# A transformer block on one core: half of x loaded on ScalarE's queue, the small vectors on GpSimd's

## The chip, the cores and the metric

The kernel runs on one core of a Trainium2 chip. The metric is the device time of one execution in microseconds, the median of several runs. TensorE multiplies matrices; VectorE, ScalarE and GpSimd work element by element; SyncE does little but issue transfers. In the profile they are PE, DVE, ACT, POOL and SP, and PEld is TensorE's weight load. Transfers between the chip's memory and the core run on 16 DMA engines; an instruction on the queue of SyncE, ScalarE or GpSimd issues each one.

## The reference

One decoder block on 256 tokens of width 2048, all in float32. A vector `c` gives six shifts, scales and gates (adaLN).

```python
mod = jax.nn.silu(c) @ w_ada[l] + b_ada[l]
sh1, sc1, g1, sh2, sc2, g2 = jnp.split(mod, 6, axis=-1)
h = modulate(rms_norm(x, norm1_g[l]), sh1, sc1)        # h * (1 + sc1) + sh1
proj = h @ w_in[l]                                     # q, k, v, gb, gc, xt
...
attn = moba_attention(q, k, v)                         # 256 tokens: one causal block
conv = gb * causal_dwconv(gc * xt, conv_w[l], conv_b[l])
mixed = jnp.concatenate([rms_norm(attn, attn_out_g[l]), rms_norm(conv, conv_out_g[l])], axis=-1)
x = x + g1 * (mixed @ w_out[l])
h2 = modulate(rms_norm(x, norm2_g[l]), sh2, sc2)
u = causal_dwconv(h2 @ w_ffn_up[l], ffn_conv_w[l], ffn_conv_b[l])
u_gate, u_up = jnp.split(u, 2, axis=-1)
x = x + g2 * ((jax.nn.silu(u_gate) * u_up) @ w_ffn_down[l])
```

The weights make up nearly all of the 320 MB that are moved: w_ada is 2048 x 12288, w_in 2048 x 6144, w_out 2048 x 2048, w_ffn_up 2048 x 11264 and w_ffn_down 5632 x 2048.

## The kernel before, in words

**Slots.** The program is a list of 205 slots. A slot is one stretch of matmuls on up to four weight blocks of 128 rows by 512 columns: slots 0 to 48 are the input projection, 49 to 64 the output projection, 65 to 204 the feed-forward part, up and down projection in turns. Each float32 weight tile `raw` is loaded by SyncE, copied to a rounded part `hi` by ScalarE (L947) and subtracted to a rest `lo` by VectorE or GpSimd (L958); TensorE multiplies both parts. This split is made two slots ahead of its use.

**Hand-made order.** Nothing is scheduled by a planner at run time: each engine runs its instructions in the order in which the program issues them, and the table `CFG` sets that order by hand. `move` and `cls` say in which slot, and at which place in it, a task stands (an evacuation, a transpose, a piece of attention); `pool` says which `lo` halves of a slot GpSimd makes (1: the first, 2: the second, 3: both, 0: none); `pool_h` names the chunks of `h` whose rest GpSimd makes; `pre`, `mid`, `after` and `carry` say how many steps of adaLN accumulation VectorE does at which place.

**adaLN.** The products with w_ada are spread over the whole program. The first 256 columns of scale and shift (`ada_init`) come first of all: TensorE multiplies each 128 x 256 block with `crep`, a replicated silu(c) (L1034), ScalarE copies the sum out, TensorE transposes it, and VectorE forms the columns A1 and B1 with the first norm's gain and the bias of adaLN, both held in `vbc`.

**The head.** `CFG["start"]` is the order of the first work. In the program's order: c is loaded on ScalarE's queue; constants and the mask are made; x is loaded in four pieces of 128 tokens x 1024 columns, 512 KB each (`xr[t][i]`, L1939, t being the half of the tokens); then the gain of the first norm (16 rows of 128) and the bias of adaLN (96 rows of 128), together `vb` (L854, called at the line after L1939); then the first weight tiles (`load_next`), in the order in which the head uses them: four 512 KB loads of scale columns, eight 256 KB loads of shift columns, then w_in. All but c go through SyncE's queue. ScalarE squares the four pieces of x in the order t = 0, then t = 1 (L1961), VectorE forms 1/rms and scales x in place (L1969), and TensorE transposes it (`xn`, L2029). `vb` is transposed by TensorE to `vbc` between two runs of warm-up matmuls (L1948), ahead of the first `ada` matmuls, and copied out by VectorE after 1/rms. The chunks of h are formed at L1624 to L1631, and the first matmuls of the input projection, `mq`, follow.

**Semaphores of transfers.** The transfers issued by SyncE and ScalarE share eight semaphores, taken in turn: the ninth transfer in the program's order waits, ahead of its issue, until the first has landed. The transfers of GpSimd have eight of their own.

Of the kernel before, what the change touches and what calls it, by code (L numbers as in the profile page):

```python
# [211 lines left out]
               63: 0,  # L212
               64: 6,
               65: 2,
# [20 lines left out]
               108: 3,  # L235
               109: 4,
               159: 2,
               171: 3},
# [56 lines left out]
                72: 0,  # L295
                83: 0},
       'pool_h': [4, 5, 6, 7, 8, 9, 10, 11, 15],
       'psum': [[0, 45]],
# [439 lines left out]
       'evac': [5, 0, 1],  # L738
       'sq': [3, 6, 0],
       'tr': [4, 7, 1],  # L740
# [38 lines left out]
               'qk_root': 0,  # L779
               'evac_out': 1},  # L780
       'la': 2,
       'h_act': True,
       'h_lag': 1,
       'hi_late': [1, 2, 3, 5, 7, 8, 9, 10, 13, 14, 15, 17, 19, 20, 21, 25, 26, 27, 32, 33, 34, 40, 49, 50, 51, 52, 55, 56,
# [3 lines left out]


@with_exitstack  # L790
def tile_block(
# [74 lines left out]
    nc.vector.memset(ones, 1.0)  # L866
    c32 = const.tile([P, P], F32, name="c32")
    nc.vector.memset(c32, 1.0 / 32.0)
    mask = const.tile([P, 384], F32, name="mask")
    nc.gpsimd.memset(mask, 0.0)  # L870
# [70 lines left out]

    def split_hi(nb):
        ts, his = [], []
        for i in range((nb + 1) // 2):
            m = min(2, nb - 2 * i) * 512
            t = take()
            act(piece(his, "hi")[:, :m], t[:, :m], AF.Copy)  # L947
            ts.append((t, m))
        halfway.append((ts, his))
# [36 lines left out]
    class Ada:  # L986


        def __init__(self, part, c0, n, pe, psum=False):
            self.part, self.c0, self.n, self.pe, self.psum = part, c0, n, pe, psum or pe  # L990
            self.rows = 2048 // n
            self.tiles = NK // self.rows
            self.nch = n // P
            self.w = min(n, 512 if self.psum else n)
            self.seen = 0
            self.out = False
            self.own = [] if [part, c0] in CFG["own"] else None

        def want(self, r):
# [12 lines left out]
        def start(self):  # L1012
# [4 lines left out]
            else:  # L1017
                self.acc = [(t4k if self.n > 512 else t2k)(what)[:, :self.n]]

        def consume(self, r, part=None):  # L1020
            if r == 0 and part != 1:
# [4 lines left out]
            for j in range(self.rows) if part is None else range(8 * part, 8 * part + 8):  # L1026
                i = self.rows * r + j
                x = j * self.n % size
                if x == 0:
                    h = take() if self.own is None else self.own.pop(0)  # L1030
                t, last = h[:, x:x + self.n], self.own is None and x + self.n == 1024
                if self.pe:
                    q = 32 * (j % 4)
                    mm(self.acc[0][q:q + 32, :], crep[:, i, :], t,  # L1034
                       start=(r == 0 and j < 4), stop=(r == self.tiles - 1 and j >= self.rows - 4),
                       tile_position=(0, q))
# [40 lines left out]
        def cols(self):  # L1077
# [3 lines left out]
            for a in range(0, self.nch, 4):  # L1081
# [5 lines left out]
                else:  # L1087
# [3 lines left out]
                    V.tensor_reduce(out=z, in_=p[:, :m * P].rearrange("p (k q) -> p k q", q=P), axis=AX.X, op=ALU.add)  # L1091
                self.finish(z, self.c0 + a, m, scale)

        def finish(self, z, c0, m, scale):
# [405 lines left out]
    def evac_down(seg, f):  # L1500
# [3 lines left out]
        for t in range(2):  # L1504
            p = mainp["D", seg, f][t]
            if seg == 0:
                dacc[t, f] = t2k(f"da{t}{f}")
# [10 lines left out]
    def gate_down(f):  # L1518
        assert all(f"ed{seg}{f}" in done for seg in range(len(SEGS) - 1)) and f"un{f}" in done
        done.add(f"gd{f}")  # L1520
        for t in range(2):
            V.tensor_tensor(out=dacc[t, f], in0=dacc[t, f], in1=gB[G2, f], op=ALU.mult)
            V.tensor_tensor(out=x1[t, f], in0=dacc[t, f], in1=x1[t, f], op=ALU.add)

    flip = [False]
# [6 lines left out]
    for seg, (ga, gb_) in enumerate(SEGS):  # L1532
# [50 lines left out]
        for f, k, n in parts:  # L1583
            def go(hi, lo, seg=seg, f=f, k=k, n=n, ka=ka, kb=kb):
                last = k + n == kb
                mm_tok(("D", seg, f), *([blk(v, j) for j in range(n)] for v in (hi, lo)), [gT[k + j] for j in range(n)], n, k == ka, last,
                       last and seg == len(SEGS) - 1)

            slots.append((w_load(w_down, k, n, [(f * 512, 512)]), n, go))
            if k + n == kb:  # L1590
# [7 lines left out]
    ready_at = {}  # L1598

    def spread_loads(g, a, span):  # L1600

        for r in range(g.tiles):
            s = a + r * span // g.tiles
            extra.setdefault(s, []).append((g, r))
        at(s + 1, g.evac)
        if g.gate():
            gates.setdefault(g.part, []).append(g)
# [34 lines left out]
    for i, (g, r) in enumerate(fill):  # L1642
        if i >= n0 + n1 + n2:
            extra.setdefault(N_OUT + (i - n0 - n1 - n2) // 2, []).append((g, r))
        if r == g.tiles - 1:
            a = N_OUT + 1 + max(0, (i - n0 - n1 - n2) // 2)
            at(a, g.evac)
            at(a + 1, g.cols)
            ready_at.update({(g.part, g.c0 + k): a + 1 for k in range(4)})
# [83 lines left out]
    def att_s(h):  # L1733
# [5 lines left out]
        s = t2k("s")[:, :384]  # L1739
        V.tensor_tensor(out=s, in0=p[:, :384], in1=mask, op=ALU.add)  # L1740
        m, z = small(2, "m"), small(2, "z")
        V.reduce_max(out=m[:, 0:1], in_=s[:, :128], axis=AX.X)
        V.reduce_max(out=m[:, 1:2], in_=s[:, 128:], axis=AX.X)
        i, j = (col("q", t, h) for t in range(2))
# [191 lines left out]
    for t in range(2):  # L1936
        xr.append([sb.tile([P, 1024], F32, tag="lo" if t else "hi", bufs=N_HL, name="xr") for _ in range(2)])
        for i in range(2):
            nc.sync.dma_start(xr[t][i], x[0, t * P:(t + 1) * P, i * 1024:(i + 1) * 1024])  # L1939
    vb, nb = rows("vb", [(by_p(norm1_g[0]), 16), (by_p(b_ada[0]), 96)], nc.sync)  # L1940
    for _ in range(N_RAW):
# [53 lines left out]
    def slot(i):  # L1995
        more = i + LA < len(slots)
        hi_late = i == N_OUT or i in CFG["hi_late"]
        if more and not hi_late:
            split_hi(slots[i + LA][1])
        now[0] = i  # L2000
# [5 lines left out]
        if more and hi_late:  # L2006
            split_hi(slots[i + LA][1])
        steps_of(CFG["pre"].get(i, 1))
# [7 lines left out]
        if i > 1:  # L2016
            slots[i][2](*splits.pop(0))
        for g, r in extra.get(i, []):
            g.consume(r)

# [106 lines left out]
```

## Time and profile before

| what | us |
| --- | --- |
| three runs, median (lowest to highest) | 1174.56 (1174.26 to 1174.75) |
| the profiled execution | 1173.49 |
| its span, first to last instruction | 1171.6 |

The profile is of one execution. Its span leaves out what lies before the first and behind the last instruction. "Busy" counts computing instructions; the issue of a transfer isn't counted. A busy TensorE needn't be at its peak, since matmuls overlap. The clock is the share of TensorE's full clock that was granted: its mean over this execution was 0.998.

A row of a timeline is start, length, engine, line, operation, tile written <- tiles read, sizes and count, and in brackets the engine's idle time before it with what ended it. A row of the chain of waits is start, length and what the end was waiting for.

### The profile page before, as it was taken

Reading aid. Unit: us, or ns where it says so; the run is one execution under the profiler, and the core shown is the slowest. Engines: PE = TensorE matmul, PEld = TensorE weight load, DVE = VectorE, ACT = ScalarE, POOL = GpSimd, SP = SyncE. Lnnn points to the kernel's source line nnn. Section 1 sums busy time; section 2 is a strip of 40 time slices with the busy share of each in tenths; the row PEclk is TensorE's granted clock in tenths of the full one; section 3 lists DMA queues with packets and bytes.
Section 4 is the critical chain, followed back from the end, with each engine's and each line's share of the span. In section 5 each row is a group of like instructions: output and inputs, shape, how many; then the busy total and the mean of one; then the engine's idle time right before and its main releaser. Section 6 shows DMA issues by size and latency. Waiting matters only on the chain.

```text
span 1171.6 us, 17108 instructions
## 1 busy us (share of the span) xinstructions
PE 1155.4 (99%) x5989; PEld 965.8 (82%) x5989; DVE 917.6 (78%) x1311; ACT 646.9 (55%) x1002; POOL 169.3 (14%) x100
## 2 busy tenths in 40 slices
PE   7999999999999999999999999999999999999998
PEld 5678888878777878888888888888888888888886
DVE  4469979997788989999999544768888897666785
ACT  4666565578566455556676444555435554445461
POOL 0768673631001021000000000000000000000000
PEclk9999999999999999999999999999999999999999
DMA  9999999995799989986465755576887877875541
GB/s 349 405 405 374 406 353 386 390 388 170 262 368 315 362 272 360 378 276 208 156 207 187 235 180 181 175 230 220 284 299 262 306 245 231 292 246 174 169 155 72
DMA packets 205382, 320.22 MB, mean 273 GB/s; under 512 B 13816, under 2 KB 112300, under 8 KB 205296
## 3 DMA queue, kind: packets, MB, share of 16 engines
q1 hardware_dynamic: 202336, 314.68, 77.2%
q10 hardware_dynamic: 2352, 4.22, 1.3%
q8 instruction: 47, 0.77, 0.3%
q14 instruction: 39, 0.32, 0.1%
q0 software_dynamic: 608, 0.23, 0.1%
HBM read 314.87 MB, written 4.21 MB: 272 GB/s over the span
## 4 chain that ended last, share of the span: by engine, by line
PE 91%; DMA 5%; DVE 3%; issue 1%; ACT 0%; POOL 0%; SPq 0%; DVEq 0%; POOLq 0%; ACTq 0%
PE z L1545 27%; PE z L1549 14%; DMA raw<-in_w_in_dram 2%; DMA raw<-in_w_ada_dram 2%; PE ada L1034 1%; PE mx L1194 1%; PE mx L1196 1%; PE mx L1195 1%; PE mk L1194 1%; DVE ada L1051 1%; PE mg L1194 1%; PE mg L1196 1%; PE mc L1194 1%; PE mq L1194 1%; PE mc L1196 1%; PE mg L1195 1%
## 5 line engine op out<-in xcount | busy, mean ns | idle before, releaser
L947 ACT ACTIVATE hi<-raw 128x1024 fp32r<-128x1024 f32 (+1 forms) x401 | 401.2, 1030 | 314.2 <-PE z L1545 92.9
L958 DVE TENSOR_TENSOR lo<-raw,hi 128x1024 fp32r<-128x1024 f32 x340 | 397.6, 1208 | 95.6 <-ACT hi L947 90.3
L1545 PE MATMUL z<-h,hi 128*128 128x512 f32 x1408 | 328.9, 390 | 0.0
L1545 PEld LDWEIGHTS z<-h,hi 128*128 128x128 f32 x1408 | 261.3, 188 | 52.6 <-DVE h L1440 0.3
L1051 DVE SCALAR_TENSOR_TENSOR ada<-raw,csil,ada 128x512 f32<-128x512 f32 (+2 forms) x215 | 189.0, 892 | 5.6 <-DMA raw<-in_w_ada_dram 2.0
L958 POOL TENSOR_TENSOR lo<-raw,hi 128x1024 fp32r<-128x1024 f32 x61 | 150.5, 2489 | 269.2 <-ACT hi L947 269.2
L1549 PEld LDWEIGHTS z<-h,lo 128*128 128x128 f32 x1408 | 174.8, 192 | 3.4
L1549 PE MATMUL z<-h,lo 128*128 128x256 f32 x1408 | 176.0, 283 | 0.0
L1110 POOL MEMSET gb<- 128x512 f32 x2 | 1.1, 526 | 491.8 <-DVE uy L1484 491.8
L1461 DVE TENSOR_TENSOR ub<-z,ub 128x256 f32<-128x256 f32 x120 | 43.8, 417 | 34.5 <-ACT ub L1458 34.4
L1458 ACT ACTIVATE ub<-z 128x256 f32<-128x256 f32 x120 | 39.7, 383 | 31.1 <-PE z L1545 31.0
L1477 ACT ACTIVATE uy<-ub,vcols 128x256 f32<-128x256 f32 x88 | 45.6, 593 | 6.8 <-DMA gr<-gs 6.7
L1482 DVE SCALAR_TENSOR_TENSOR uy<-ub,vcols,uy 128x255 f32<-128x255 f32 x88 | 42.1, 479 | 5.7 <-ACT uy L1477 5.6
L1484 DVE SCALAR_TENSOR_TENSOR uy<-ub,vcols,uy 128x254 f32<-128x254 f32 x88 | 42.5, 483 | 3.1
L1493 ACT ACTIVATE gh<-uy 128x512 fp32r<-128x512 f32 x22 | 13.9, 630 | 40.6 <-DVE uy L1491 40.6
L1487 ACT ACTIVATE uy<-uy 128x512 f32<-128x512 f32 x22 | 13.9, 633 | 37.2 <-DVE uy L1484 37.2
L1034 PE MATMUL ada<-raw,crep 128*32 128x512 f32 (+1 forms) x224 | 27.1, 525 | 3.2 <-DMA raw<-in_w_ada_dram 2.7
L1494 DVE TENSOR_TENSOR gl<-uy,gh 128x512 fp32r<-128x512 f32 x22 | 15.2, 693 | 17.9 <-ACT gh L1493 17.9
L1194 PE MATMUL mk<-hi,h 128*128 128x512 f32 x64 | 25.8, 403 | 0.0
L1194 PE MATMUL mq<-hi,h 128*128 128x512 f32 x64 | 25.3, 395 | 0.4 <-ACT pa_g L1214 0.4
L1194 PE MATMUL mg<-hi,h 128*128 128x512 f32 x64 | 25.7, 401 | 0.0
L1194 PE MATMUL mx<-hi,h 128*128 128x512 f32 x64 | 25.3, 396 | 0.0
(574 smaller groups left out, 1922.8 us busy)
## 6 DMA issues: line engine op xcount, KB each, us to landing
raw<-in_w_ada_dram SPq DMA_DIRECT2D x180, 512.0 KB, 6.8
raw<-in_w_ffn_up_dram SPq DMA_DIRECT2D x352, 256.0 KB, 4.7
raw<-in_w_in_dram SPq DMA_DIRECT2D x95, 512.0 KB, 7.1
raw<-in_w_ffn_down_dram SPq DMA_DIRECT2D x76, 512.0 KB, 4.7
raw<-in_w_out_dram SPq DMA_DIRECT2D x32, 512.0 KB, 6.1
raw<-in_w_ada_dram SPq DMA_DIRECT2D x24, 256.0 KB, 6.6
raw<-in_w_ffn_down_dram SPq DMA_DIRECT2D x24, 256.0 KB, 3.8
xr<-in_x_dram SPq DMA_DIRECT2D x4, 512.0 KB, 5.4
```

The source lines that it names most:

```text
L947: act(piece(his, "hi")[:, :m], t[:, :m], AF.Copy)
L958: (nc.gpsimd if pool in (i + 1, 3) else V).tensor_tensor(out=piece(los, "lo")[:, :m], in0=t[:, :m], in1=hi[:, :m].bitcast(F32), op=ALU.sub ...
L1034: mm(self.acc[0][q:q + 32, :], crep[:, i, :], t, start=(r == 0 and j < 4), stop=(r == self.tiles - 1 and j >= self.rows - 4), tile_positio ...
L1051: V.scalar_tensor_tensor(out=self.acc[n], in0=v, scalar=csil[:, i:i + 1], in1=acc, op0=ALU.mult, op1=ALU.add)
L1194: mm(o, a, hi[k], start=(first and k == 0 and not seeded), stop=False, skip_group_check=True)
L1458: act(c[ft // 2][:, (ft % 2) * 256:(ft % 2) * 256 + 256], zp[grp][ft][:, 256:], AF.Copy)
L1461: V.tensor_tensor(out=d, in0=zp[grp][ft][:, :256], in1=d, op=ALU.add)
L1477: act(y, b, AF.Identity, bias=fcols[3][:, i:i + 1], scale=fcols[2][:, i:i + 1])
L1482: V.scalar_tensor_tensor(out=y[:, 1:], in0=b[:, :255], scalar=fcols[1][:, i:i + 1], in1=y[:, 1:], op0=ALU.mult, op1=ALU.add)
L1484: V.scalar_tensor_tensor(out=y[:, 2:], in0=b[:, :254], scalar=fcols[0][:, i:i + 1], in1=y[:, 2:], op0=ALU.mult, op1=ALU.add)
L1545: mm(zp[grp][ft], blk(hi, j)[:, ft * P:(ft + 1) * P], h2T[k + j], start=k + j == ks[0], stop=k + j == ks[1] - 1)
L1549: mm(zp[grp][ft][:, :256], blk(lo, j)[:, ft * P:(ft + 1) * P], h2T[k + j][:, :256], start=False, stop=False)
```

## The change

Two issues of x (the second 128 tokens) go from SyncE's queue to ScalarE's, and the two issues of `vb` to GpSimd's. In the same change a number of entries of `CFG` are different, and the code gains branches which the values of `CFG` leave unused (`sets`, `tail`, `lag` empty, `ttr` false). The core of it:

```diff
     for t in range(2):
         xr.append([sb.tile([P, 1024], F32, tag="lo" if t else "hi", bufs=N_HL, name="xr") for _ in range(2)])
         for i in range(2):
-            nc.sync.dma_start(xr[t][i], x[0, t * P:(t + 1) * P, i * 1024:(i + 1) * 1024])
-    vb, nb = rows("vb", [(by_p(norm1_g[0]), 16), (by_p(b_ada[0]), 96)], nc.sync)
+            (nc.scalar if CFG["xq"] and t else nc.sync).dma_start(
+                xr[t][i], x[0, t * P:(t + 1) * P, i * 1024:(i + 1) * 1024])
+    vb, nb = rows("vb", [(by_p(norm1_g[0]), 16), (by_p(b_ada[0]), 96)], nc.gpsimd if CFG["xq"] else nc.sync)
...
+       'xq': True,
+       'lag': {},
+       'sets': [],
+       'tail': [],
+       'ttr': False}
...
-    c32 = const.tile([P, P], F32, name="c32")
+    c32 = const.tile([P, 32], F32, name="c32")
```

The entries of the order table:

```diff
 mid
-               64: 6,
+               148: 2,
 pool
+                153: 3,
+                187: 1,
+                188: 1,
+                189: 1,
+                200: 3},
-       'pool_h': [4, 5, 6, 7, 8, 9, 10, 11, 15],
+       'pool_h': [5, 6, 7, 8, 9, 10, 11, 15],
 after
-                 'evac_in q1 True': 3,
+                 'evac_in q1 True': 1,
 move
+                'evac 2 0': (0, 2),
-                'evac_c 3 1': (0, 1),
+                'evac_c 3 1': (0, 0.5),
-                'ffn_cols': (5, 2),
+                'ffn_cols': (4, 2),
+                'up_conv 10': (0, -2),
-       'sq': [3, 6, 0],
+       'sq': [3, 4, 0],
 hi_late: 66 taken out
```

`mid` is the number of accumulation steps between the two halves of a slot's `lo`; `sq` sets the slot in which a part of the new x is squared (the second part two slots earlier); `ffn_cols` turns the small vectors of the feed-forward part into columns, one slot earlier; `hi_late` lists the slots whose `hi` is made behind the slot's first tasks.

More of the change, by code (lines that the diff above doesn't have):

```diff
@@ L779 @@
                'qk_root': 0,
[L780 removed]
+               'evac_out': 1,
+               'cols_set': -1},
        'la': 2,
@@ L866, in tile_block @@
     nc.vector.memset(ones, 1.0)
-    c32 = const.tile([P, P], F32, name="c32")
+    c32 = const.tile([P, 32], F32, name="c32")
     nc.vector.memset(c32, 1.0 / 32.0)
+    pick = {}
+    for v in (1.0, 1.0 / 32.0):
+        if CFG["sets"]:
+            pick[v] = const.tile([P, 39], F32, name=f"pick{int(1 / v)}")
+            nc.gpsimd.memset(pick[v], 0.0)
+            nc.gpsimd.memset(pick[v][:, 7:8], v)
     mask = const.tile([P, 384], F32, name="mask")
@@ L940, in piece, with split_hi @@
         return t[-1]
-    def split_hi(nb):
+    gated = {}
+    def split_hi(n):
+        nb = slots[n][1]
         ts, his = [], []
@@ L1018, in start, with hold @@
                 self.acc = [(t4k if self.n > 512 else t2k)(what)[:, :self.n]]
+        def hold(self, r):
+            tiles = self.rows * self.n // (1024 if self.own is None else 512)
+            self.held[r] = [take() if self.own is None else self.own.pop(0) for _ in range(tiles)]
         def consume(self, r, part=None):
@@ L1029, in consume @@
                 if x == 0:
-                    h = take() if self.own is None else self.own.pop(0)
+                    src = self.held.get(r, self.own)
+                    h = take() if src is None else src.pop(0)
                 t, last = h[:, x:x + self.n], self.own is None and x + self.n == 1024
@@ L1092, in cols, with cols_set @@
                 self.finish(z, self.c0 + a, m, scale)
+        def cols_set(self):
+            groups = self.set
+            p = bank(f"adas{self.part}_{self.c0}", full=False)
+            parts = [(g, a) for g in groups for a in range(0, g.nch, 4)]
+            for n, (g, a) in enumerate(parts):
+                assert g.out
+                flush(g)
+                e = pick[1.0 / 32.0 if g.pe else 1.0][:, 7 - n:39 - n]
+                m = min(4, g.nch - a)
+                for q in range(m):
+                    mm(p[32 * q:32 * q + 32, :P], e, g.chunk(a + q), start=n == 0, stop=n == len(parts) - 1,
+                       tile_position=(0, 32 * q))
+            r = t1k("adar")[:, :P]
+            act(r, p[:, :P], AF.Copy)
+            p = bank(f"adat{self.part}_{self.c0}", full=False)
+            nc.tensor.transpose(p[:, :P], r, ident)
+            for n, (g, a) in enumerate(parts):
+                m = min(4, g.nch - a)
+                g.finish(p[:, n:n + 32 * m - 31:32], g.c0 + a, m, 1.0)
         def finish(self, z, c0, m, scale):
@@ L1505, in evac_down @@
             p = mainp["D", seg, f][t]
-            if seg == 0:
+            if seg == len(SEGS) - 1 and f in CFG["tail"]:
+                y = t2k(f"d{f}{t}")
+                V.tensor_copy(y[:, :256], p[:, :256])
+                act(y[:, 256:], p[:, 256:], AF.Copy)
+                for eng, a in ((nc.sync, 0), (nc.scalar, 256)):
+                    eng.dma_start(out[0, t * P:(t + 1) * P, f * 512 + a:f * 512 + a + 256], y[:, a:a + 256])
+            elif seg == 0:
                 dacc[t, f] = t2k(f"da{t}{f}")
@@ L1523, in gate_down, with seed_down @@
             V.tensor_tensor(out=x1[t, f], in0=dacc[t, f], in1=x1[t, f], op=ALU.add)
+    def seed_down(f):
+        assert f"gd{f}" in done
+        key = "D", len(SEGS) - 1, f
+        whole[key] = None
+        mainp[key] = [bank(f"ms{f}{t}", keep=True, seed=True) for t in range(2)]
+        for t in range(2):
+            act(mainp[key][t], x1[t, f], AF.Copy)
     flip = [False]
@@ L1587, in go @@
                        last and seg == len(SEGS) - 1)
+            if seg == len(SEGS) - 1 and f in CFG["tail"]:
+                gated[len(slots)] = f
+                if k == ka:
+                    put(len(slots) - 1, CFG["cls_seed"], seed_down, f)
             slots.append((w_load(w_down, k, n, [(f * 512, 512)]), n, go))
@@ L1598, in tile_block, with in_set @@
     ready_at = {}
+    held_until = {}
+    sets = {(part, c0): n for n, e in enumerate(CFG["sets"]) for part, c0 in e}
+    filling = {}
+    def in_set(g, s):
+        n = sets.get((g.part, g.c0))
+        if n is None:
+            return False
+        filling.setdefault(n, []).append((s, g))
+        if len(filling[n]) < len(CFG["sets"][n]):
+            return True
+        s, gs = max(s for s, _ in filling[n]), [g for _, g in filling[n]]
+        gs[0].set = gs
+        at(s + 2, gs[0].cols_set)
+        ready_at.update({(g.part, g.c0 + k): s + 2 for g in gs for k in range(g.nch)})
+        return True
     def spread_loads(g, a, span):
@@ L1604, in spread_loads @@
             extra.setdefault(s, []).append((g, r))
+            lag = CFG["lag"].get(f"{g.part} {g.c0}", 0)
+            if lag:
+                s += lag
+                held_until.setdefault(s, []).append((g, r))
         at(s + 1, g.evac)
+        if in_set(g, s):
+            return
         if g.gate():
@@ L1739, in att_s @@
         s = t2k("s")[:, :384]
-        V.tensor_tensor(out=s, in0=p[:, :384], in1=mask, op=ALU.add)
         m, z = small(2, "m"), small(2, "z")
-        V.reduce_max(out=m[:, 0:1], in_=s[:, :128], axis=AX.X)
-        V.reduce_max(out=m[:, 1:2], in_=s[:, 128:], axis=AX.X)
+        if CFG["ttr"]:
+            for t, a, b in ((0, 0, 128), (1, 128, 384)):
+                V.tensor_tensor_reduce(out=s[:, a:b], in0=p[:, a:b], in1=mask[:, a:b], scale=1.0, scalar=NEG,
+                                       op0=ALU.add, op1=ALU.max, accum_out=m[:, t:t + 1])
+        else:
+            V.tensor_tensor(out=s, in0=p[:, :384], in1=mask, op=ALU.add)
+            V.reduce_max(out=m[:, 0:1], in_=s[:, :128], axis=AX.X)
+            V.reduce_max(out=m[:, 1:2], in_=s[:, 128:], axis=AX.X)
         i, j = (col("q", t, h) for t in range(2))
@@ L1998, in slot @@
         if more and not hi_late:
-            split_hi(slots[i + LA][1])
+            split_hi(i + LA)
         now[0] = i
@@ L2006, in slot @@
         if more and hi_late:
-            split_hi(slots[i + LA][1])
+            split_hi(i + LA)
         steps_of(CFG["pre"].get(i, 1))
@@ L2018, in slot @@
         for g, r in extra.get(i, []):
+            if f"{g.part} {g.c0}" in CFG["lag"] and (g, r) not in fill:
+                g.hold(r)
+            else:
+                g.consume(r)
+        for g, r in held_until.get(i, []):
             g.consume(r)
```

9 lines of the change are left out of this document (8 added, 1 removed), and 6 rows, old and new, of tables.

## The prediction

> **What bounds the kernel now.** I read the page's busy shares and its chain first, then the chain in order of time, then the stretches, then the queues in the first 20 us.
>
> ```profile
> PE 1155.4 (99%) x5989; PEld 965.8 (82%) x5989; DVE 917.6 (78%) x1311; ACT 646.9 (55%) x1002; POOL 169.3 (14%) x100
> PE 91%; DMA 5%; DVE 3%; issue 1%; ACT 0%; POOL 0%; SPq 0%; DVEq 0%; POOLq 0%; ACTq 0%
> 40.50:1168.00 1127.50, 1124.27 (x5781) 945.47 (x5779) 899.17 (x1267) 627.00 (x969) 162.12 (x89) 1.00 0.78 271
> 0.00:40.50 40.50, 31.15 (x210) 20.31 (x211) 17.95 (x44) 19.93 (x33) 7.17 (x12) 0.96 1.00 361
> ```
>
> The last two rows are stretches: bounds, length, then the busy time (and count) of PE, weight loads, DVE, ACT, POOL, the clock, the DMA share, GB/s. From 40.5 us to 1168 us TensorE is busy for 1124.27 of 1127.50 us, so 3.23 us is idle there. In the first 40.5 us, 9.35 us is idle, with the DMA share at 1.00. So the kernel has two parts: a **head** that waits for data, and a **body** in which TensorE runs through. A microsecond gained in the head moves the whole body. The chain of waits (start, length, what) says what the head waits for:
>
> ```profile
> 1.65 6.39 DMA xr<-in_x_dram
> 8.06 7.54 DMA raw<-in_w_ada_dram
> 15.62 6.01 DMA raw<-in_w_in_dram
> 21.65 8.38 DMA raw<-in_w_ada_dram
> 30.05 6.57 DMA raw<-in_w_ada_dram
> 36.66 3.14 PE ada L1034 x16
> ```
>
> Five transfers, end to end, each issued within 0.02 us of the landing of the one before. SyncE's queue issues a load only when an older one has landed; the third piece of x, issued at 1.65, lands at 8.04 and lets a load of w_ada go. From 36.66 on the chain is TensorE. The change acts on the first link.
>
> **The change, part by part.** *The issue.* SyncE's queue in the first microseconds (start, length, engine, what):
>
> ```profile
> 0.74 1.81 SPq L1939 DMA_DIRECT2D xr<-in_x_dram  x4
> 2.59 0.93 SPq L854 DMA_DIRECT2D vb<-in_norm_g_dram  x1
> 3.57 0.46 SPq L854 DMA_DIRECT2D vb<-in_b_ada_dram  x1
> 4.08 11.19 SPq L1007 DMA_DIRECT2D raw<-in_w_ada_dram  x12
> ```
>
> Two of the four x issues and both issues of vb leave this queue, so the first w_ada load goes out where the third x issue stood: at 1.65 in place of 4.08, **2.43 us earlier**. Two of the w_ada loads behind it also lose the x or vb transfer that they waited for. Issue time is not data, though. The stretches show what the DMA engines did with the time:
>
> ```profile
> 0.00:2.00 2.00, 0.00 (x0) 0.00 (x0) 0.31 (x2) 0.81 (x1) 1.32 (x9) 1.00 0.19 18
> 2.00:4.00 2.00, 0.00 (x0) 0.00 (x0) 0.00 (x0) 0.47 (x1) 0.28 (x2) 1.00 0.69 197
> 4.00:6.00 2.00, 1.37 (x6) 1.36 (x7) 0.60 (x2) 0.85 (x2) 0.00 (x0) 1.00 1.05 414
> 6.00:8.00 2.00, 2.00 (x12) 2.00 (x11) 0.00 (x0) 1.96 (x5) 0.00 (x0) 1.00 1.00 297
> 10.00:20.00 10.00, 7.74 (x75) 3.21 (x75) 5.43 (x17) 2.59 (x7) 0.00 (x0) 1.00 1.09 388
> ```
>
> The last column is GB/s. From 10 us on the engines are full at 388 GB/s and stay so through the head; the bytes that the head needs don't change. So the head can move only by bytes carried sooner in the first 8 us. Against 388 GB/s, 2 to 4 us loses (388 − 197)/388 × 2 = 0.98 us, and 6 to 8 us loses (388 − 297)/388 × 2 = 0.47 us. The first 2 us lose 1.91 us, but nothing is issued before 0.74, and I count none of it as won. The thin stretch of 2 to 4 us has all of x issued by 2.55, on one queue, with the engines 69% busy. A second queue that feeds the same engines from about 1.2 us should fill most of it. No trace shows this, so the bounds are wide: nothing (the engines themselves start slowly) and 2.43 us (the whole shift of the issue). I take three quarters of both losses, 0.75 × 1.45 = 1.09, or **1.1 us**, since the third row shows the engines at 414 GB/s right after, with x alone still moving.
>
> A rule of the Trainium skill speaks against this. "DMA: Bandwidth & Descriptors", section "Issuing engines are not separate DMA queues", says that transfers started by different engines run on the same 16 DMA engines and interleave, and that starting them from several engines saves only the time of the sequencer. By that rule alone the sum would be near nothing; the share of 0.69 at 2 to 4 us says the engines still had room, so the trace doesn't settle it.
>
> *What TensorE can use of it.* On the other branch of the head stands x itself:
>
> ```profile
> 5.36 1.28 ACT L1954 ACT_TABLE_LOAD   x1
> 6.77 1.04 ACT L1961 ACTIVATE j<-xr 128x1024 f32<-128x1024 f32 x1
> 10.29 1.06 ACT L1961 ACTIVATE j<-xr 128x1024 f32<-128x1024 f32 x1
> 9.94 0.29 PE L878 MATMUL pv_vbc<-ident,vb 112*128 112x112 f32 x1 [0.49 <-DMA vb<-in_b_ada_dram]
> 10.07 0.62 PE L1948 MATMUL warm<-ones,ident 128*128 128x128 f32 x4
> 13.36 0.81 PE L2029 MATMUL xn<-ident,xr 128*128 128x128 f32 x4 [0.49 <-DVE xr L1969]
> 14.92 0.64 PE L1034 MATMUL ada<-raw,crep 128*32 128x256 f32 x8 [0.18 <-DMA raw<-in_w_ada_dram]
> 16.87 4.14 PE L1034 MATMUL ada<-raw,crep 128*32 128x256 f32 x32
> 16.87 0.58 PEld L1034 LDWEIGHTS ada<-raw,crep 128*32 128x32 f32 x12 [0.17 <-issue]
> 20.38 0.14 PEld L1034 LDWEIGHTS ada<-raw,crep 128*32 128x32 f32 x4 [0.53 <-DMA raw<-in_w_ada_dram]
> ```
>
> The four squares of x run back to back from 6.77 (one each 1.17 us), begun when a table load ends, not when x lands; so the normalized x reaches TensorE at 13.36 whatever x does, unless a piece lands late. Behind it the shift columns' matmuls start at 16.87, or 16.69 without the 0.18 us of DMA wait at 14.92. Twelve weight loads take 0.58 there when the data is present, so the last four of 32 could start at 16.69 + 28 × 0.048 = 18.04 in place of 20.38: TensorE can take in up to **2.3 us**. My 1.1 fits under this cap. The first w_in tile and the w_ada loads up to 36.62 stand in the same full stream and move with it.
>
> *Where the moved issues go.* The rows are ScalarE's and GpSimd's first work, and two on later loads by GpSimd (shortest, median and longest issue in ns; us to landing):
>
> ```profile
> 0.73 0.42 ACTq L854 DMA_DIRECT2D vc<-in_c_dram  x1
> 5.13 0.21 ACT L1953 ACTIVATE csil<-ccol 128x16 f32<-128x16 f32 x1 [2.66 <-DVE ccol L880]
> 1.74 0.54 POOL L872 TENSOR_SCALAR_AFFINE_SELECT mask<-mask 128x128 f32<-128x128 f32 x2
> 34.94 11.82 POOL L958 TENSOR_TENSOR lo<-raw,hi 128x1024 fp32r<-128x1024 f32 x5 [32.66 <-ACT hi L947]
> L854 POOL DMA_DIRECT2D v<-in_norm_g_dram x1: 653/653/653, 66.6 to 66.6; - x1
> DMA to landing us min/median/max: 4.8/5.2/5.5
> ```
>
> ScalarE's two x issues cost 2 × 0.45 (a quarter of SyncE's 1.81 each) after its own load of c, beginning near 1.19, and push its first table load, of 1.28 like the one at 5.36, to end near 3.4. ScalarE is idle until 5.13, so this is hidden; without that cover it would cost 0.9. GpSimd issues vb after its mask, from about 2.3 us; later loads of the same kind show the price. At 0.65 an issue, the second starts at 2.95 and vb lands by 2.95 + 5.5 = 8.5, where TensorE now waits for it until 9.94. What stands in TensorE's order between vb and 13.36 is 0.29 + 0.62 (four warm matmuls) + 2 × 0.64; vb is harmless until 13.36 − 2.19 = 11.2. GpSimd's next work is at 34.94, after 32.66 us without any. Gain from vb itself: 0, as the work behind it waits for w_ada and x.
>
> *The order edits.* The table of pieces that GpSimd subtracts gains one for each of the slots 187 to 189 and two for 153 and for 200, seven in all; one chunk of h goes from GpSimd to VectorE; some tasks and accumulation steps of slots 18 to 66, 125 and 148 move within their slot or by one or two. The entry removed for slot 64 is never read (that slot returns before it). The unused branches (sets, tail, lag, ttr) issue nothing; c32 shrinks from 128 to 32 columns.
>
> ```profile
> L958 DVE TENSOR_TENSOR lo<-raw,hi 128x1024 fp32r<-128x1024 f32 x340 | 397.6, 1208 | 95.6 <-ACT hi L947 90.3
> L958 POOL TENSOR_TENSOR lo<-raw,hi 128x1024 fp32r<-128x1024 f32 x61 | 150.5, 2489 | 269.2 <-ACT hi L947 269.2
> 980.00:1168.00 188.00, 187.01 (x944) 159.66 (x944) 131.23 (x179) 85.72 (x118) 0.00 (x0) 1.00 0.58 186
> 1145.29 0.63 ACT L947 ACTIVATE hi<-raw 128x512 fp32r<-128x512 f32 x1 [1.61 <-PE m('D', 3, 1)1_11131 L1196]
> 1149.17 0.39 PE L1194 MATMUL m('D', 3, 3)0_11295<-hi,gh 128*128 128x512 f32 x1
> ```
>
> A piece takes 2.49 us on GpSimd and 1.21 on VectorE, but is made two slots before it is used. The tightest is slot 200: its second, half-wide piece can start at 1145.92 and ends near 1147.4 (half of 2.49), 1.7 us ahead of its matmuls. So the edits cost 0; if all seven stood on the path they would cost 7 × 1.28 = 9.0 us. What they can win is at most the 3.23 us of TensorE idle time behind 40.5 us. I take 0: none of the idle time is shown to end with one of the moved tasks.
>
> **The sum.** 1.1 us of the profiled execution's 1173.49 (span 1171.6 and 1.9 around it). That execution lies 1.07 us below the median of the runs, 1174.56, so I take the gain from the median: 1174.56 − 1.1 = 1173.46, say **1173.4**. A measurement of this kernel can tell about 0.2%, or 2.35 us, from no change, so this counts as the same.
>
> **The rivals.** *First, the start is the engines' own.* If 2 to 4 us stay thin with two queues, w_ada's earlier issue only lengthens the line behind x, and what is left is at most part of the 0.47 us: about 1174.3. For it: the third row, where the rate reaches 414 with nothing changed but time. Against it: the 69%. The same result comes if the last piece of x, now interleaved with w_ada, lands after 10.29: from there each microsecond late pushes 13.36 and eats the gain.
>
> *Second, the whole shift comes through.* If the 2.43 us of earlier issue arrive as earlier landings, the cap gives 2.3 us, and if a quarter of the later idle time also goes (0.25 × 3.23 = 0.8), the time is 1174.56 − 3.1 = 1171.5. For it: five landings in a row each release the next issue, so that an early first link is handed on. Against: a full stream at 388 GB/s hands on bytes, not issue times.
>
> *Third, slower: a GpSimd piece that comes late.* The place is slots 187 to 200, where seven subtractions go to an engine that takes twice as long. The price is 1.28 us for each that TensorE waits for; from three on the path (3.8 less the 1.1 of the head) the kernel is 2.7 us slower, and at four the time is 1174.56 + 5.1 − 1.1 = 1178.6. It decides when a hi piece ends later than 1.7 us after where it ends now (slot 200). For it: GpSimd does nothing from 980 us to 1168 now, so no row shows such a piece there. Against: the lead of two slots.
>
> The change doing less than it says isn't likely: the code moves the two x issues and vb without condition.
>
> **How the numbers follow.** Forecast (0.5 to 2.2 us won) 0.52; first rival 0.15; second 0.25; third 0.08. The first two of these are within 0.2%, the second rival is faster by over 0.2%, the third slower: faster 0.25, same 0.67, slower 0.08. The range leaves out the third and about half of the second rival: from 1171.2 (the cap of 2.3, 0.8 of later idle time, and 0.3, by which the runs differ from their median) to 1175.2 (no gain, and half of one piece late).
>
> **What would show it.** The first w_ada issue on SyncE's queue at about 1.65; 2 to 4 us well above 197 GB/s; x's squares still from 6.8 us; vb's transpose near 9.5 without a DMA wait; the last shift matmuls and the ada matmuls that begin at 36.66 all about 1.1 us earlier; from 40.5 us on the same 3.2 us of idle time. The forecast is wrong if 2 to 4 us stay at 197, if squares wait for x, or if TensorE's idle time behind 40.5 us changes by more than 1 us.

## The result, and the profile after

| | us | runs |
| --- | --- | --- |
| before, median (lowest to highest) | 1174.47 (1172.72 to 1174.75) | 6 |
| changed, median (lowest to highest) | 1183.09 (1180.92 to 1184.23) | 6 |
| the profiled execution of the changed kernel | 1183.94, span 1182.2 | 1 |

The changed kernel is slower by 0.73%: the ratio is 1.0073, with a 95% interval from 1.0059 to 1.0086, or 8.6 us. That is small, but clear of the scatter of the runs. The forecast was 1173.4 and its range ended at 1175.2.

The page of the changed kernel first: busy time of the engines in us, and the shares of the chain that ended last.

```profile
PE 1158.2 (98%) x5989; PEld 966.6 (82%) x5989; DVE 920.3 (78%) x1305; ACT 646.5 (55%) x1002; POOL 186.4 (16%) x108
PE 87%; DMA 5%; DVE 5%; issue 1%; ACT 0%; SPq 0%; ACTq 0%; DVEq 0%
```

The span grew by 10.6 us (1182.2 − 1171.6), while TensorE's busy time grew by 2.8; the other 7.8 us are idle time. The stretches of the changed kernel say where (bounds, length, then the busy time and count of PE, weight loads, DVE, ACT, POOL, the clock, the DMA share, GB/s; the share adds up the time of all packets, so it passes 1 where packets of one DMA engine overlap):

```profile
2.00:4.00 2.00, 0.00 (x0) 0.00 (x0) 0.00 (x0) 1.28 (x1) 1.46 (x4) 1.00 0.78 195
4.00:6.00 2.00, 1.43 (x7) 1.43 (x8) 0.60 (x2) 0.92 (x2) 0.00 (x0) 1.00 1.01 391
6.00:8.00 2.00, 2.00 (x11) 2.00 (x11) 0.00 (x0) 1.96 (x5) 0.00 (x0) 1.00 1.02 362
10.00:20.00 10.00, 6.41 (x63) 2.42 (x62) 5.43 (x17) 2.53 (x7) 0.00 (x0) 1.00 1.10 348
20.00:37.00 17.00, 15.60 (x104) 11.41 (x104) 8.99 (x18) 8.50 (x15) 0.96 (x1) 1.00 1.06 379
40.00:80.00 40.00, 40.00 (x186) 27.80 (x185) 20.38 (x35) 24.88 (x38) 29.97 (x22) 0.97 1.05 390
120.00:160.00 40.00, 37.36 (x170) 30.37 (x169) 38.33 (x56) 21.57 (x30) 27.34 (x15) 1.00 1.05 383
200.00:240.00 40.00, 38.62 (x171) 31.65 (x169) 34.14 (x45) 21.76 (x41) 17.29 (x8) 1.00 1.05 390
240.00:280.00 40.00, 37.18 (x173) 29.84 (x174) 34.97 (x57) 26.57 (x63) 11.97 (x9) 0.96 0.93 309
280.00:1178.40 898.40, 896.38 (x4735) 761.67 (x4733) 709.70 (x985) 485.22 (x740) 37.50 (x19) 1.00 0.73 242
```

The same stretches of the kernel before, as far as the prediction didn't show them:

```profile
20.00:37.00 17.00, 15.03 (x104) 11.26 (x100) 10.02 (x20) 9.61 (x16) 2.06 (x1) 1.00 1.06 399
40.00:80.00 40.00, 40.00 (x188) 29.35 (x189) 22.39 (x37) 27.96 (x42) 31.60 (x22) 0.99 1.04 407
80.00:120.00 40.00, 40.00 (x184) 33.18 (x184) 33.85 (x53) 23.61 (x31) 32.35 (x17) 1.00 1.02 383
120.00:160.00 40.00, 40.00 (x184) 33.01 (x183) 38.16 (x54) 21.19 (x29) 26.60 (x14) 1.00 1.04 395
160.00:200.00 40.00, 39.65 (x177) 32.33 (x176) 31.45 (x39) 25.02 (x47) 23.06 (x10) 1.00 0.97 362
200.00:240.00 40.00, 40.00 (x178) 33.15 (x177) 36.82 (x50) 22.82 (x43) 20.34 (x8) 1.00 1.03 394
240.00:280.00 40.00, 39.13 (x198) 31.84 (x197) 32.58 (x63) 29.49 (x64) 10.13 (x8) 1.00 0.84 301
280.00:1168.00 888.00, 886.00 (x4683) 753.02 (x4681) 703.90 (x977) 476.91 (x719) 18.53 (x11) 1.00 0.73 243
```

Two things are to be seen. From 280 us on TensorE's idle time is the same, 2.02 us after and 2.00 before: nothing is lost in the feed-forward part, where GpSimd's added pieces stand. And from 10 us on the DMA engines are as busy as before (share 1.10 against 1.09, 1.06 against 1.06) but carry **fewer bytes**: 348 in place of 388 GB/s, 379 in place of 399. The same busy time for fewer bytes means that the packets take longer.

The trace records every packet of a transfer with its size and duration. For the weight loads they say this (mean ns of one packet):

| packet | before | changed | difference |
| --- | --- | --- | --- |
| 1 KB, 8 to 20 us | 46.0 | 51.0 | 5.0 |
| 2 KB, 40 to 80 us | 85.1 | 88.8 | 3.7 |
| 4 KB, 40 to 80 us | 160.1 | 164.9 | 4.8 |

Before, the shortest tenth, the median and the longest tenth of the 1 KB packets are all 46 ns; after, the median is 51 and the longest tenth begins at 59, while the shortest tenth is still at 46. So a packet takes some 4 to 5 ns more on the mean, whatever its size, but not every packet does. And this holds only where the DMA engines are full: from 280 to 1100 us the medians are the same before and after (84 ns at 2 KB, 159 at 4 KB) and so, nearly, are the means (95.3 and 95.6 ns, 180.0 and 179.4).

Where TensorE falls behind is read from the start of the n-th matmul in the one trace less its start in the other (both kernels have 5989). In us, at the time in the kernel before, for the changed kernel and for three experiments told of below:

| at | changed | c32 narrow only | queues only | order entries only |
| --- | --- | --- | --- | --- |
| 21 | 1.1 | 1.8 | 0.1 | 0.2 |
| 69 | 2.8 | 3.1 | −0.7 | −0.2 |
| 146 | 3.8 | 3.1 | −0.7 | 0.1 |
| 160 | 5.8 | 4.8 | 0.3 | 1.3 |
| 228 | 5.0 | 4.3 | −0.5 | 1.4 |
| 254 | 10.4 | 8.2 | 0.1 | 1.9 |
| 1124 | 10.4 | 8.2 | 0.1 | 1.8 |

All of the loss comes ahead of 254 us, in the head and the input projection. Each column is one execution, and small distances in it are scatter: the kernel with the late order entries alone (below) runs the same instructions as the kernel before, in the same order on every engine and queue, up to 396 us, and its distance is −0.5 at 146 us and 3.0 at 254; that of the kernel with a delay at 353 us (below) is 0.2 and −0.4.

A part of the loss is the granted clock. The row from 240 to 280 us has 0.96 in place of 1.00: the trace shows half the clock for 3.4 us from 261.0 us on, which is 1.7 of the 10.4 us, and the kernel with the narrow `c32` alone (8.2 us late) has no such interval there. In all traces together there are four such intervals between 100 and 300 us, and each begins within 1.5 us of the end of a stall of 1.9 to 2.3 us of TensorE; not every such stall has one behind it. The mean clock of the six runs of the changed kernel is 0.993 to 0.998, with a median of 0.996; in 27 runs of the kernel before it is 0.995 to 1.000, with a median of 0.999. Taken at its most, 0.003 of 1183 us, the clock is some 3.5 us of the loss (an estimate). That the stalls bring the low clock on fits these rows, but no run separates the two.

### The profile page after: what moved, and what is told of

It reads as the page before. It is cut to its first block, busy times and chain, and to the rows that moved or that the text cites. A ratio compares the mean times of both kernels' runs of the same rounds, so it can differ in the third digit from the quotient of the medians.

```text
span 1182.2 us, 17115 instructions
## 1 busy us (share of the span) xinstructions
PE 1158.2 (98%) x5989; PEld 966.6 (82%) x5989; DVE 920.3 (78%) x1305; ACT 646.5 (55%) x1002; POOL 186.4 (16%) x108
## 4 chain that ended last, share of the span: by engine, by line
PE 87%; DMA 5%; DVE 5%; issue 1%; ACT 0%; SPq 0%; ACTq 0%; DVEq 0%
PE z L1611 27%; PE z L1615 14%; DMA raw<-in_w_ada_dram 3%; DVE ada L1083 2%; DMA raw<-in_w_in_dram 2%; PE ada L1066 1%; PE mg L1246 1%; PE mx L1246 1%; PE mg L1248 1%; PE mx L1248 1%; PE mg L1247 1%; PE mx L1247 1%; PE mc L1248 1%; PE mc L1246 1%; PE mc L1247 1%
## 5 line engine op out<-in xcount | busy, mean ns | idle before, releaser
L984 DVE TENSOR_TENSOR lo<-raw,hi 128x1024 fp32r<-128x1024 f32 (+1 forms) x333 | 392.0, 1215 | 99.8 <-ACT hi L973 92.0
L984 POOL TENSOR_TENSOR lo<-raw,hi 128x1024 fp32r<-128x1024 f32 x68 | 167.4, 2480 | 923.8 <-ACT hi L973 914.3
L1083 DVE SCALAR_TENSOR_TENSOR ada<-raw,csil,ada 128x512 f32<-128x512 f32 (+2 forms) x215 | 193.0, 911 | 6.9 <-DMA raw<-in_w_ada_dram 3.2
L1123 DVE TENSOR_REDUCE adaz<-adac 128x4 f32<-128x512 f32 (+1 forms) x18 | 11.4, 634 | 19.8 <-PE adac L1121 17.2
L1246 PE MATMUL mv<-hi,h 128*128 128x512 f32 x64 | 25.3, 396 | 1.4 <-ACT pa_k L1266 1.4
```

What stands on the lines that cost most here:

```text
L984: (nc.gpsimd if pool in (i + 1, 3) else V).tensor_tensor(out=piece(los, "lo")[:, :m], in0=t[:, :m], in1=hi[:, :m].bitcast(F32), op=ALU.sub ...
L1083: V.scalar_tensor_tensor(out=self.acc[n], in0=v, scalar=csil[:, i:i + 1], in1=acc, op0=ALU.mult, op1=ALU.add)
L1246: mm(o, a, hi[k], start=(first and k == 0 and not seeded), stop=False, skip_group_check=True)
```

## Experiments

**Theory.** The change has a part that the prediction passed over: `c32` loses 96 columns of float32, 384 bytes in each partition. It is allocated early, so every tile behind it lies 384 bytes lower, the `raw` tiles among them, into which the weights are loaded. By a count of the tiles these stood on multiples of 512 bytes, so now they start 128 bytes past one. The traces show no addresses; the experiments below test the count. The theory is that a load whose destination isn't aligned, that is, doesn't start at such a multiple, takes longer. The rivals are that the other queues slow the stream, and that the order entries do.

### Each part by itself

Four kernels share their runs of the kernel before. First, the changed kernel with the wide `c32`:

```diff
-    c32 = const.tile([P, 32], F32, name="c32")
+    c32 = const.tile([P, P], F32, name="c32")
```

> The changed kernel with c32 back at 128 columns (512 bytes a partition), nothing else. With c32 at 32 columns every tile behind it in the core's memory lies 384 bytes lower, and the raw tiles start at 128 past a multiple of 512 in place of at a multiple. Theory A (placement): the transfers into raw were slow because of this; the 1 KB packets of 10 to 20 us are back at one length, 46 ns, the rate at 388 GB/s, and the time is 1172 to 1174.5 us. Theory B (queues: the early transfers by GpSimd or ScalarE disturb the DMA engines): the placement is nothing; 1181 to 1184 us. Theory C (order edits stall TensorE between 140 and 265 us): also 1181 to 1184 us, but with full transfer rates.

Second, the kernel before with the narrow `c32` and nothing else (the same line the other way):

> The kernel before with c32 at 32 columns, nothing else. Theory A: 1180 to 1184 us, with the rate of 10 to 20 us near 350 GB/s. Theories B and C: 1174.5 us, within 0.1%.

Third, the queues alone, in the kernel before:

```diff
-            nc.sync.dma_start(xr[t][i], x[0, t * P:(t + 1) * P, i * 1024:(i + 1) * 1024])
-    vb, nb = rows("vb", [(by_p(norm1_g[0]), 16), (by_p(b_ada[0]), 96)], nc.sync)
+            (nc.scalar if t else nc.sync).dma_start(xr[t][i], x[0, t * P:(t + 1) * P, i * 1024:(i + 1) * 1024])
+    vb, nb = rows("vb", [(by_p(norm1_g[0]), 16), (by_p(b_ada[0]), 96)], nc.gpsimd)
```

> The kernel before with the two x issues on ScalarE's queue and vb on GpSimd's, c32 wide and the order table as before. Theory A: the queues by themselves are what the forecast says or less, 1173.4 to 1174.5 us. Theory B: 1181 us or more. Theory C: 1173.4 to 1174.5 us.

Fourth, the changed kernel with an unused tile of 128 bytes behind the narrow `c32`, which puts the tiles behind it on multiples of 256 bytes (not of 512):

```diff
     c32 = const.tile([P, 32], F32, name="c32")
+    const.tile([P, 32], F32, name="pad")
```

> The changed kernel with an unused constant of 32 columns behind c32, so that the raw tiles start at a multiple of 256, though not of 512. Theory A with a limit at 256 bytes: 1172 to 1174.5 us, as with c32 wide. Theory A with a limit at 512: 1180 to 1184 us. Theories B and C: 1181 to 1184 us.

And the order entries alone (the changed kernel with the wide `c32` and `'xq': False`):

> The changed kernel with c32 wide and x and vb on SyncE's queue again: only the order table differs from the kernel before. If the 0.13% that the changed kernel with c32 wide loses comes from the order edits: 1175 to 1176 us, with TensorE waiting for more than 1 us near 128 us or 152 us. If it comes from the two queues together with the edits: 1174 us, within 0.1%.

| kernel | median us | ratio | 95% interval |
| --- | --- | --- | --- |
| changed, c32 wide again | 1175.09 | 1.0013 | 1.0004 to 1.0021 |
| before, c32 narrow only | 1181.24 | 1.0058 | 1.0045 to 1.0070 |
| before, queues only | 1173.98 | 0.9999 | 0.9990 to 1.0008 |
| changed, padded to 256 | 1175.40 | 1.0013 | 1.0004 to 1.0022 |
| before, order entries only | 1175.41 | 1.0013 | 1.0005 to 1.0022 |

The stretches from 10 to 20 and from 20 to 37 us, first of the kernel before with the narrow `c32`, then of the changed kernel with the wide one, then of the padded one:

```profile
10.00:20.00 10.00, 7.56 (x65) 3.27 (x67) 5.43 (x17) 2.66 (x7) 0.00 (x0) 0.83 1.10 349
20.00:37.00 17.00, 16.18 (x108) 11.50 (x108) 8.31 (x17) 7.78 (x14) 0.25 (x1) 1.00 1.06 379
```

```profile
10.00:20.00 10.00, 7.26 (x71) 2.71 (x70) 5.43 (x17) 2.58 (x7) 0.00 (x0) 1.00 1.09 389
20.00:37.00 17.00, 15.21 (x104) 11.40 (x104) 10.27 (x21) 9.88 (x16) 2.35 (x2) 1.00 1.06 399
```

```profile
10.00:20.00 10.00, 7.28 (x73) 2.80 (x71) 5.43 (x17) 2.63 (x7) 0.00 (x0) 1.00 1.09 388
20.00:37.00 17.00, 15.28 (x104) 11.26 (x100) 10.09 (x20) 9.67 (x16) 2.12 (x1) 1.00 1.06 399
```

The rate follows the address alone: 348 or 349 and 379 GB/s where `c32` is narrow without a pad, 387 to 389 and 399 or 400 where it is wide or padded, whichever queues and order entries the kernel has. The padded kernel keeps the narrow `c32` and everything else of the change, so the width of `c32` as such is not the cause. The three parts sum to 0.58 − 0.01 + 0.13 = 0.70%, against 0.73% measured for the whole.

### Which tiles, and which alignment

Three more edits of the kernel before. In the first, two unused tiles around the first load put the `raw` tiles alone 128 bytes past a multiple of 512, and everything behind them where it was:

```diff
-    for _ in range(N_RAW):
+    sb.tile([P, 32], F32, tag="pad1", bufs=1, name="pad1")
+    load_next()
+    sb.tile([P, 96], F32, tag="pad2", bufs=1, name="pad2")
+    for _ in range(N_RAW - 1):
         load_next()
```

> The kernel before with 128 unused bytes a partition ahead of the ten raw tiles and 384 behind them: raw alone starts at 128 past a multiple of 512, all other tiles stand at multiples of 512 as before. Theory A1 (the destination of the transfers counts): nearly all transfers go into raw, so most of the loss of the narrow c32 is there, 1178 to 1182 us, with 350 GB/s at 10 to 20 us. Theory A2 (the operands of the engines count, and the transfers only follow): 1174 us, within 0.2%.

In the second, `pad2` has 32 columns and another 32 stand behind `c32`: `raw` lies on multiples of 256, everything else is 128 off.

> The kernel before with 128 unused bytes ahead of all work tiles and 128 more on either side of raw: raw starts at a multiple of 256, everything else 128 past one (hi, lo, x, the tiles of 512 and 256 columns). Theory A1: 1173.5 to 1175.5 us, as only x, eight early loads of w_ada and a few small ones go elsewhere than into raw, with full rate. Theory A2: 1178 to 1182 us.

In the third, 16 columns behind `c32` put all tiles 64 bytes off:

```diff
     c32 = const.tile([P, P], F32, name="c32")
+    const.tile([P, 16], F32, name="pad")
```

> The kernel before with an unused constant of 16 columns: every work tile starts 64 past a multiple of 512. If any start off 256 costs the same, as one more access for each packet would: 1180 to 1184 us, 350 GB/s at 10 to 20 us. If the loss grows with the distance: 1176 to 1179 us. If 64-byte placement is enough: 1174 us.

| kernel before, with | median us | ratio | 95% interval |
| --- | --- | --- | --- |
| raw alone 128 off | 1180.61 | 1.0065 | 1.0047 to 1.0083 |
| all but raw 128 off | 1175.34 | 1.0014 | 1.0005 to 1.0022 |
| all 64 off | 1180.04 | 1.0054 | 1.0041 to 1.0067 |

The stretches of the kernel with `raw` alone 128 off, and then of the one with all but `raw` off:

```profile
10.00:20.00 10.00, 7.05 (x71) 3.15 (x71) 5.43 (x17) 2.73 (x7) 0.00 (x0) 1.00 1.10 366
20.00:37.00 17.00, 15.26 (x104) 11.26 (x100) 9.46 (x19) 9.01 (x15) 1.47 (x1) 1.00 1.06 400
40.00:80.00 40.00, 40.00 (x186) 28.80 (x185) 21.42 (x35) 26.75 (x40) 30.31 (x23) 0.99 1.05 392
```

```profile
10.00:20.00 10.00, 7.66 (x71) 3.14 (x71) 5.43 (x17) 2.41 (x6) 0.00 (x0) 1.00 1.10 374
20.00:37.00 17.00, 15.09 (x102) 11.25 (x100) 9.48 (x19) 9.02 (x15) 1.49 (x1) 1.00 1.06 386
40.00:80.00 40.00, 40.00 (x187) 28.83 (x184) 21.50 (x35) 27.71 (x42) 31.36 (x23) 0.97 1.05 406
```

They complement each other. Some of the first adaLN loads go into tiles of another kind (`raw2`, under the tag of `t2k`), the rest and all of the projection's go into `raw`. With `raw` alone off, 10 to 20 us is slow (366 GB/s), 20 to 37 is not (400), and from 40 us, when nearly all loads go into `raw`, the rate is 392 where the kernel before has 407. With the others off, the head is slow (374, 386) and 40 to 80 us is not (406). Of the two, the one with `raw` off has nearly the whole loss, 0.65%; the one whose stream is slow in the **head alone** is at 0.14% (0.05 to 0.22). An offset of 64 costs as much as one of 128 (its 1 KB packets take 51.0 ns in 8 to 20 us); a shift by 256 costs no transfer time. That is the border that the runs show; offsets below 64 and between 128 and 256 weren't tried.

What the thinner stream does to TensorE is the same in all four kernels whose `raw` tiles are off: it waits ahead of the same matmuls, `mg` near 155 us (1.56 to 1.92 us), `mv` near 240 (0.71 to 1.99) and `as` near 261 (2.23 to 2.26). The wait at `mv` is in none of the other traces. In the changed kernel it is this row:

```profile
240.07 0.50 PE L1246 MATMUL mv<-hi,h 128*128 128x512 f32 x1 [1.45 <-ACT pa_k L1266]
```

"DMA: Bandwidth & Descriptors" of the Trainium skill, section "How a descriptor splits into AXI transactions", says that a transfer's piece is cut at multiples of 256 bytes, and that the first transaction of one that doesn't start on such a multiple starts at the multiple below, with bytes fetched and not used. It says so of the read. By that rule a piece of 1 KB that starts 64 or 128 bytes past a multiple takes five transactions in place of four (an estimate from the page's rule). The border of 256 bytes, and an offset of 64 that costs as much as one of 128, fit this. But one more transaction for every packet would be a fixed cost, and a tenth or more of the packets take their old time in the full stretches, half of them from 280 us on. So which tiles and which offsets slow the loads is shown; what happens inside the DMA engines, and on the write into the core's memory, stays open.

### Does a delay move the end?

The prediction said that a microsecond gained in the head moves the whole body. In the kernel before, one group of four adaLN transposes is made eight times over (same result), once at 88 us and once at 353 us:

```diff
-                    for k in range(m):
+                    turn.append(1)
+                    for k in list(range(m)) * (8 if len(turn) == 5 else 1):
                         nc.tensor.transpose(p[:, k * P:(k + 1) * P], self.chunk(a + k), ident)
```

> The kernel before, with the four transposes at 87.8 us made eight times over (same result): 28 more of 0.109 us, so TensorE loses 3.0 us there. If TensorE alone sets the end behind 40.5 us, as the prediction had it, the time grows by 3.0 us (0.26%). If the input projection is bound by transfers as well, the loads run ahead meanwhile and a part of the later stalls goes (0.63 us at 162 us and 1.11 at 252 in the kernel before): the time grows by 1.3 us or less (0.11%).

The other has 11 in place of 5:

> The same 28 transposes more, at 352.9 us, behind the stretch in which the DMA share is over 1. Both theories: TensorE is the bound there, so the time grows by 3.0 us (0.26%), or by 1.7 if the stall of 1.35 us at 431.7 us takes a part of it. The difference from the same delay at 88 us is what tells the two stretches apart.

The times were 1177.05 (ratio 1.0032, 1.0020 to 1.0045) and 1176.95 us (1.0029, 1.0019 to 1.0040), against 1173.6 before: some 3.4 us for the 3.0 added, at both places. So the input projection doesn't absorb a delay. A stretch of the kernel with the delay at 88 us, and a row of its timeline, fit this:

```profile
80.00:120.00 40.00, 40.00 (x199) 33.68 (x198) 30.89 (x46) 21.12 (x29) 27.83 (x16) 1.00 0.95 336
155.86 0.50 PE L1196 MATMUL mg<-hi,h 128*128 128x512 f32 x1 [1.19 <-ACT mg L1205]
```

The transfers don't run ahead while TensorE is late: 336 GB/s where the kernel before has 383 in the same stretch. A load needs a free `raw` tile, which is free when the work on it is done; the likely reading is that the loads stop with TensorE. Afterwards both go on at the old pace. The stall at 155.86 isn't in the profile of before, but the kernel with the queues alone has one there too (0.86 us), so it says nothing of the delay. My theory that the projection hides part of a delay fell.

### What the order entries cost

To find their 0.13%, four of them were set back (`pool_h`, `evac_in q1 True`, `evac 2 0` and `ffn_cols` as before; `c32` wide, queues as before). In the traces the entries that stay change the order of an engine's instructions from 396 us on, and the four act at 91 to 144 us, later than the expectation says:

> The order edits alone, without those that act ahead of 60 us (the chunk 4 of h, the three adaLN steps after an evacuation, one evacuation, one slot of the feed-forward columns): what stays are the entries of slots 125 to 200. If the 0.13% (1.5 us) of the order edits come from GpSimd's added pieces at slots 153 to 200 or the tasks of slots 125 to 148, the time stays at 1.0013. If they come from the early entries, which fall into the stretch that the transfers bound and where the loss is seen (a stall of 1.2 us at 151.7 us), the ratio is 1.000 and that stall is gone. If it is only one way of many in which the stalls of that stretch fall, the ratio lies between and the stall is at another place.

It took 1174.24 us, ratio 1.0006 (0.9997 to 1.0014). That lies between the two answers and can't be told from either. The stall near 151 us that the kernel with all order entries shows (1.16 us) is gone from its profile (TensorE busy for 39.99 of 40 us from 120 to 160), but 3.22 us are idle from 240 to 280, where the kernel before has 0.87:

```profile
120.00:160.00 40.00, 39.99 (x184) 32.90 (x183) 38.37 (x52) 21.18 (x29) 26.97 (x14) 1.00 1.04 394
240.00:280.00 40.00, 36.78 (x186) 29.74 (x185) 32.62 (x57) 26.47 (x54) 10.87 (x8) 1.00 0.87 301
```

Up to 396 us this kernel does the same work in the same order as the kernel before, so these 3.22 us aren't the work of any entry: the profiled execution took 1176.37 us, the longest of the eleven, and the stalls of this part vary from one execution to the next. Which entry costs the 0.13% stays open.

## Why the prediction was wrong, step by step

**The step that failed** is in "The order edits": "The unused branches (sets, tail, lag, ttr) issue nothing; c32 shrinks from 128 to 32 columns", with the cost 0 for all of it. That a smaller tile issues nothing is right, but it moves the address of every tile behind it. By itself it costs 0.58% (0.45 to 0.70), 6.8 us of 1174.47, which is four fifths of the loss (the stalls that follow, and what the clock takes behind them, included). It had no price in the sum and no bound in the range.

**The size of it.** "From 10 us on the engines are full at 388 GB/s and stay so through the head" was taken as a constant, and it fell to 348. The prediction's body was "TensorE runs through", read from the 3.23 us of idle time behind 40.5 us. That was true, but not the whole of it: up to 240 us the DMA share is between 0.97 and 1.04 as well (the stretches of 40 us), so TensorE and the transfers were both near their limit, and a stream that is up to 4% thinner in these stretches (390 against 407 GB/s from 40 to 80 us) becomes idle time. In the changed kernel, in the stretch that corresponds, it is 8.86 us:

```profile
40.50:1178.40 1137.90, 1129.04 (x5789) 947.49 (x5785) 902.02 (x1261) 626.53 (x969) 179.21 (x96) 1.00 0.79 269
```

The prediction had named this as a sign ("if TensorE's idle time behind 40.5 us changes by more than 1 us"), but not the cause. From 280 us on the share is 0.73, and there the packets are hardly slower (the medians are the same) and TensorE's idle time is as before.

**The earlier issue** came as said and was worth little. SyncE's first load of w_ada goes out at 1.66 (predicted 1.65). A row of SyncE's timeline in the changed kernel:

```profile
1.66 14.22 SPq L1034 DMA_DIRECT2D raw<-in_w_ada_dram  x12
```

The same row of the kernel with the queues alone, whose packets are at full speed:

```profile
1.64 13.63 SPq L1007 DMA_DIRECT2D raw<-in_w_ada_dram  x12
```

And from the changed kernel again, the chain of waits, then the issues of this line:

```profile
4.45 2.92 SPq L1034
7.42 1.80 SPq L1034
9.27 7.73 DMA raw<-in_w_ada_dram
17.01 6.41 DMA raw<-in_w_in_dram
23.44 8.61 DMA raw<-in_w_ada_dram
32.06 7.05 DMA raw<-in_w_ada_dram
39.15 2.58 PE ada L1066 x12
```

```profile
L1034 SPq DMA_DIRECT2D raw<-in_w_ada_dram x204: 328/368/2925, 1.7 to 963.8; - x102
```

Twelve issues that took 11.19 us before take 14.22 now, and 13.63 with the queues alone. There they end at 1.64 + 13.63 = 15.27, where they ended before too (4.08 + 11.19): all of the 2.43 us is handed back within them. The median issue takes 368 ns, but the two from 4.45 on in the changed kernel take 2.92 and 1.80. The longest issue of this line is 2.85 to 3.11 us in the four kernels with the moved queues and under 2 us in the others; that SyncE stands because so much is outstanding already is a guess.

**The thin stretch did not fill.** From 2 to 4 us the rate stayed at 195 GB/s (before: 197). That is the prediction's first rival, "the start is the engines' own". The stretch from 6 to 8 us did fill: 350 to 377 GB/s in the four kernels with the moved queues, 272 to 313 in the nine others. So the term of 1.1 us was too large. With the queues alone the last head load came 0.7 us earlier; but among the kernels whose tiles all stand on multiples of 256 its row starts at 36.30 to 36.99 in the four others without moved queues, and at 36.21 and 36.35 in the two others with them, so the gain is nearer 0.4 (the difference of the means). These are rows of the kernel before with the queues alone, two stretches and the `ada` matmuls, which began at 36.66 before:

```profile
2.00:4.00 2.00, 0.00 (x0) 0.00 (x0) 0.00 (x0) 1.28 (x1) 1.43 (x4) 1.00 0.80 195
6.00:8.00 2.00, 2.00 (x12) 2.00 (x11) 0.00 (x0) 1.96 (x5) 0.00 (x0) 1.00 1.02 377
35.95 2.65 PE L1034 MATMUL ada<-raw,crep 128*32 128x256 f32 x16 [0.86 <-DMA raw<-in_w_ada_dram]
```

**"A microsecond gained in the head moves the whole body"** holds for time lost: a delay of 3.0 us at 88 us moved the end by 3.4. For time gained it stays open. The queues' ratio, 0.9999, has an interval from 0.9990 to 1.0008, or from 1.2 us gained to 0.9 lost, and a gain near 0.4 us can't be told from none in it; the 0.7 us that the table has at 146 us and not at 254 is within the scatter of one execution. So the size of the queues' own part of the forecast isn't refuted by the times, only not seen. The rule "Issuing engines are not separate DMA queues" of "DMA: Bandwidth & Descriptors" (the Trainium skill), by which the sum was near nothing, agrees with the queues' measured 0.9999.

**x and vb** behaved as said. The squares start at 6.70 and the transposes of x at 13.29 (before: 6.77 and 13.36). vb's transpose ran at 9.26 (predicted near 9.5), but behind a DMA wait of 0.27 us, since the landing took 6.1 us, not the 5.5 taken as the longest. It harmed nothing, well ahead of 11.2:

```profile
6.70 1.04 ACT L2063 ACTIVATE j<-xr 128x1024 f32<-128x1024 f32 x1
9.26 0.29 PE L897 MATMUL pv_vbc<-ident,vb 112*128 112x112 f32 x1 [0.27 <-DMA vb<-in_b_ada_dram]
13.29 0.81 PE L2136 MATMUL xn<-ident,xr 128*128 128x128 f32 x4
```

**The order entries** were costed at 0 and measure 0.13% (0.05 to 0.22), some 1.5 us, ahead of 254 us. The third rival, late GpSimd pieces at slots 187 to 200, did not happen: the distance to the kernel before is 10.4 us at 254 us and still 10.4 at 1124. In that rival's working a half of 2.49 us behind 1145.92 ends at 1147.2, not 1147.4, so the piece had 2.0 us to spare, not 1.7; nothing hangs on it.

## What to carry to other kernels

A change of a tile's size is a change of every address behind it. Before costing it at nothing, see whether the destinations of the large loads stay on multiples of 256 bytes; a pad of 128 bytes brought back all that the misplacement cost here. When transfers and TensorE are both near their limit in a stretch, "TensorE is busy" doesn't mean that only TensorE counts: read the DMA share and the GB/s of the stretch together, since the same share at fewer GB/s is the sign of slower packets. And before a stall of one profile is put down to an edit, compare the order of the instructions ahead of it: where it is the same, the stall is scatter.

## What was unexpected of the hardware

- Where the DMA engines are full, a load into tiles 64 or 128 bytes past a multiple of 256 (by the count of the tiles) costs 4 to 5 ns per packet on the mean: 46.0 to 51.0 ns at 1 KB, 388 to 348 GB/s from 10 to 20 us. Shifted by 256 bytes the rate is the full 388. Where they aren't full (a share of 0.73 from 280 us on), the median packet takes its old time.
- An issue on SyncE's queue took 2.92 us here, against a median of 0.37; the profile shows it as time of the queue in the chain.
- From 2 to 4 us the DMA engines carried 195 to 201 GB/s in the kernels with x on two queues (share 0.78 to 0.84) and 184 to 225 with x on one (0.69 to 0.81). Why they start so slowly stays open.
- TensorE's clock was halved for 3.4 us right behind a stall of 2.26 us (at 261.0 us in the changed kernel), which cost 1.7 us more.
